# One pinned order for the turn from projection to attention, the last rotation on GpSimd, and first `aT` tiles in memory of their own

## The chip, the cores and the metric

The kernel runs on one core of a Trainium2 chip. The metric is the device time of one execution in microseconds (us). The engines are named as the profile names them: PE is TensorE's matmul, PEld its weight load, DVE is VectorE, ACT is ScalarE, POOL is GpSimd and SP is SyncE, which here only issues DMAs.

## What is computed

One layer of a diffusion backbone with 1024 latent tokens and 256 context tokens of width 1024, all in float32. A combined input projection feeds two groups of heads, retention and differential attention; their outputs go through one output projection, and a gated MLP with a small convolution follows. The change concerns the start of the differential attention. Its queries get a rotation by position, and each of the 4 heads has two score maps, whose softmaxes are subtracted:

```python
def apply_rope(x, cos, sin):
    half = x.shape[-1] // 2
    x1, x2 = x[..., :half], x[..., half:]
    ...
    return jnp.concatenate([x1 * cs - x2 * sn, x1 * sn + x2 * cs], axis=-1)
...
    def attend(qb):
        s = jnp.einsum('bhmqd,bhmkd->bhmqk', qb, k).astype(jnp.float32) * scale
        p = jax.nn.softmax(s, axis=-1)
        a = p[:, :, 0] - lam * p[:, :, 1]
        return jnp.einsum('bhqk,bhke->bhqe', a.astype(v.dtype), v)
...
    n = of * lax.rsqrt(jnp.mean(of * of, axis=-1, keepdims=True) + EPS)
```

The last line is the norm of each attention output over its 128 values.

## The kernel before, in words

Products at full precision are made of three passes (`passes`, L132 to L134): a high and a low part of each operand, high with high, high with low, low with high, gathered in one PSUM tile.

The input projection is made block by block. Its last block, the queries of the differential attention, goes through `transposed`: for each head and each half of the 1024 tokens, one PSUM tile `pl` (128 features x 512 tokens) is gathered from 8 x 3 = 24 matmuls, and `rotated` turns it: four ACT copies of 32 rows put the swapped halves into `xb` (L443), DVE multiplies the tile by the cosine into `xa` (L446) and `xb` by the sine (L447) and adds them (L448). Then `split_store` casts the sum into its high part on ACT (L434), takes the low part on DVE (L435), both in `xhl`, and SP stores them to `dq_d` in device memory (L436). `xa`, `xb` and `xhl` come from a pool named `er`. The last two tiles, both of head 3, are called qa (first half of the tokens) and qb (second half) here. Head 0's queries have been stored long before and are loaded back as `qhl` (L974), its keys as `ks` (L979) and its values as `va` (L982), all issued on POOL.

Attention has 32 units, 4 heads x 8 tiles of 128 queries. The operations of a unit are methods of `Unit`, with one letter each: S, for either of two maps (S1 before S0), makes six matmuls of scores into a PSUM tile `pA` (L890); M reduces them to a minimum on DVE (`mt`, L893), E takes the exponential on ACT with its sum (`p`, `sa`, L897). R and C on DVE work out the ratio of the two sums and combine the two maps (L905). T turns the combined map in three groups, 0, 1 and 2, of four, four and two PE transposes into `pt` (L910), K copies each group to `aT` on ACT (L916), V multiplies it by the values into `pv` (L922). O copies the result to `oa` (L926), Q squares it on ACT (L931) and makes `e` on POOL (L933); f ends the norm's factor on DVE (L936) and with a power on POOL (`ssa`, L937), n scales `oa` on ACT (L940), and Y, h and l turn and split it into `yT`. `pt`, `pv` and Y's `pty` share two PSUM banks (tag "s"), so a T can start only when an earlier tile of theirs has been copied out. `aT`, `oa`, `e`, `ssa` come from a pool `at`.

What sets the order: the numbers of `TAU` place each operation of a unit in periods of one unit, the loop issues them in that order, and `in_order` pins PE, DVE, ACT and SP to the order in which the instructions are written; the order on POOL is left to a scheduler. The turn stands ahead of this loop: S1 to C of unit 0 (`EARLY`) and the tiles qa and qb are written one after the other and not pinned, so the scheduler mixes them. The pool `at` is opened when the projection's pools are closed, and lies partly in memory in which `er` was. Each head's keys go in turn to `ak0` and `ak1`, both allocated ahead of the turn.

## Time and profile before

| what | us |
|---|---|
| median of 3 runs | 1398.27 (1397.23 to 1399.22) |
| the profiled execution | 1400.12 |
| its span in the trace | 1398.3 |
| PE busy in the span | 1369.1 |
| input projection and retention end, attention begins | about 450 to 480 |
| first `pv` matmul (unit 0) | 480.18 |

The profile is of one execution, of which each instruction has a start and a duration in us from the span's start. The clock named PEclk is the share of full speed that TensorE was granted. An idle time is put down to what ended it.

### The profile page before, as it was taken

To read this page: it belongs to the slowest core of one execution; us is meant where nothing else is said; L and a number is where in the kernel's file an instruction comes from. 1 tells how busy PE (TensorE), PEld (TensorE's weight loads), DVE (VectorE), ACT (ScalarE), POOL (GpSimd) and SP (SyncE) were. 2 spreads that over 40 slices of the span, in tenths; PEclk is the share of its full clock that TensorE was granted. 3 is DMA by queue.
4 is the path that set the end of the run, shared out by engine and by line. 5 is a ranking of instruction groups with operands and counts; after the bars stand their busy time and mean duration, and the time that the engine had idled before them with its cause. 6 is when DMAs were issued, how large, how long until landed. Compare 5 with 4: busy or idle time off the path is not lost.

```text
span 1398.3 us, 19669 instructions
## 1 busy us (share of the span) xinstructions
PE 1369.1 (98%) x7028; PEld 1148.4 (82%) x7028; DVE 1013.7 (72%) x1516; ACT 740.9 (53%) x1414; POOL 336.0 (24%) x379
## 2 busy tenths in 40 slices
PE   8999999999999899999999999999999999999997
PEld 6788888788888799998887778888888888888886
DVE  5867756523466898886357998877777777998756
ACT  5546444303466789987036545554455555455433
POOL 1310002501446223411101243233322230033003
PEclk9999999999999999999999999999999999999999
DMA  9467987876679578632221223323233225953324
GB/s 383 154 210 246 309 264 247 263 239 185 191 220 228 163 171 181 139 91 75 105 98 45 91 106 113 110 93 113 98 113 113 76 90 211 392 195 102 133 98 150
DMA packets 107114, 230.88 MB, mean 165 GB/s; under 512 B 9541, under 2 KB 42821, under 8 KB 105097
## 3 DMA queue, kind: packets, MB, share of 16 engines
q1 hardware_dynamic: 98888, 204.73, 42.8%
q0 software_dynamic: 8128, 24.91, 8.0%
q8 instruction: 55, 0.90, 0.3%
q14 instruction: 43, 0.34, 0.1%
HBM read 165.37 MB, written 64.23 MB: 164 GB/s over the span
## 4 chain that ended last, share of the span: by engine, by line
PE 48%; DVE 3%; issue 1%; DMA 1%; ACT 0%; POOLq 0%; POOL 0%; DVEq 0%; ACTq 0%
PE c L133 5%; PE chain L132 5%; PE chain L133 5%; PE c L134 5%; PE c L132 5%; PE chain L134 5%; PE third L132 3%; PE third L133 3%; PE third L134 3%; PE po L134 2%; PE po L133 2%; PE po L132 2%; PE second L132 1%; PE second L133 1%; PE second L134 1%; DVE wlo L1064 1%
## 5 line engine op out<-in xcount | busy, mean ns | idle before, releaser
L132 PE MATMUL pl<-hT,whi 128*128 128x512 f32 x256 | 107.5, 420 | 0.0
L134 PE MATMUL chain<-T,wlo 128*128 128x512 f32 x264 | 103.0, 390 | 2.0 <-DVE wlo L1064 2.0
L132 PE MATMUL chain<-T,whi 128*128 128x512 f32 x264 | 103.0, 390 | 1.3 <-ACT ua L1317 1.3
L133 PE MATMUL chain<-T,whi 128*128 128x512 f32 x264 | 102.8, 389 | 0.0
L134 PE MATMUL pl<-hT,wlo 128*128 128x512 f32 x256 | 100.5, 392 | 0.0
L133 PE MATMUL pl<-hT,whi 128*128 128x512 f32 x256 | 100.2, 392 | 0.0
L893 DVE TENSOR_REDUCE mt<-pA 128x1 f32<-128x1280 f32 x64 | 95.4, 1490 | 4.1 <-PE pA L890 3.6
L890 PE MATMUL pA<-ks,qhl 128*128 128x512 f32 (+1 forms) x384 | 90.8, 372 | 2.5 <-ACT p L897 2.5
L443 ACT ACTIVATE xb<-pl 32x512 f32<-32x512 f32 (+1 forms) x96 | 56.7, 590 | 64.2 <-PE pl L134 45.1
L134 PE MATMUL c<-whi,ghl 128*128 128x512 f32 x232 | 90.4, 390 | 0.0
L132 PE MATMUL c<-whi,ghl 128*128 128x512 f32 x232 | 90.3, 389 | 0.0
L133 PE MATMUL c<-wlo,ghl 128*128 128x512 f32 x232 | 90.3, 389 | 0.0
L1212 POOL TENSOR_TENSOR cmb<-wrb 128x512 f32<-128x512 f32 x20 | 28.3, 1414 | 249.5 <-DMA wrb<-w_up 135.2
L897 ACT ACTIVATE p<-pA,mt 128x1280 f32<-128x1280 f32 x64 | 85.4, 1335 | 2.4 <-issue 1.3
L132 PE MATMUL pn<-whi,hT 128*128 128x512 f32 x192 | 85.7, 446 | 0.0
L1063 ACT CAST whi<-cmb 128x512 fp32r<-128x512 f32 x62 | 38.6, 622 | 81.3 <-PE chain L133 63.0
L890 PEld LDWEIGHTS pA<-ks,qhl 128*128 128x128 f32 x384 | 68.4, 192 | 14.4 <-ACT p L897 3.0
L134 PE MATMUL pn<-whi,hT 128*128 128x512 f32 x192 | 76.3, 398 | 1.0 <-POOL hT L608 1.0
L922 PE MATMUL pv<-va,aT 128*128 128x128 f32 x640 | 76.9, 275 | 0.1
L133 PE MATMUL pn<-wlo,hT 128*128 128x512 f32 x192 | 75.9, 396 | 0.0
L922 PEld LDWEIGHTS pv<-va,aT 128*128 128x128 f32 x640 | 74.0, 192 | 0.7 <-DVE yT L951 0.3
L1063 ACT CAST whi<-wra 128x512 fp32r<-128x512 f32 x55 | 33.9, 621 | 71.2 <-PE third L133 42.5
(324 smaller groups left out, 3901.9 us busy)
## 6 DMA issues: line engine op xcount, KB each, us to landing
raw<-w_in SPq DMA_DIRECT2D x32, 512.0 KB, 5.7
wm<-w_mod SPq DMA_DIRECT2D x32, 512.0 KB, 4.8
wra<-w_up SPq DMA_DIRECT2D x24, 512.0 KB, 3.3
wrb<-w_up SPq DMA_DIRECT2D x23, 512.0 KB, 3.5
W<-w_down SPq DMA_DIRECT2D x44, 256.0 KB, 6.2
ad<-s SPq DMA_DIRECT2D x20, 512.0 KB, 3.3
wra<-ad SPq DMA_DIRECT2D x20, 512.0 KB, 3.4
wrb<-ad SPq DMA_DIRECT2D x18, 512.0 KB, 3.7
```

Of the source, the lines that this page charges most:

```text
L132: mm(ps, lh, rh, start=first, stop=False, skip_group_check=more)
L133: mm(ps, lh, rl, start=False, stop=False, skip_group_check=more)
L134: mm(ps, ll, rh, start=False, stop=last, skip_group_check=more)
L443: nc.scalar.activation(xb[q * blk : (q + 1) * blk, :], pt[o : o + blk, :], AF.Copy, scale=scale)
L890: mm(self.pa[m][:, c0:c1], self.q[:, i, m, qs], self.k[:, m, c0:c1], start=(i == 0), stop=(i == 1))
L893: nc.vector.tensor_reduce(out=self.mt[:, m : m + 1], in_=self.pa[m][:, :LK], axis=AX.X, op=ALU.min)
L897: nc.scalar.activation(self.p[m], self.pa[m][:, :LK], AF.Exp, scale=-1.0, bias=self.mt[:, m : m + 1], accum_out=self.s[:, m : m + 1])
L922: mm(self.pv, self.aT[:, c, :], self.v[:, c, :], start=(c == 0), stop=(c == NKT - 1))
L1063: nc.scalar.copy(hi, src)
L1064: nc.vector.tensor_tensor(out=lo, in0=src, in1=r32(hi), op=ALU.subtract)
L1212: nc.gpsimd.tensor_tensor(out=s1, in0=b1, in1=b2, op=ALU.add)
```

## The change

The turn gets an order written out by hand. Units 0, 1 and 2 are created ahead of it, `begin` issues operations of a unit there, and the loop later leaves out what has begun. A class `LastQueries` holds the steps of qa and qb singly: `products` for some of the 8 steps of the gathering, `swapped`, `cosine`, `sine`, `high`, `low`, `store` as before, and two new ones. `copied` takes the whole tile to `xa` in one ACT copy; `rotated_on_gpsimd` swaps the halves with four SP DMAs from `xa` to `xb`, of 32 x 512 floats (64 KB) each, and does the rest in five POOL operations of 128 x 512. qa is rotated as before on ACT and DVE, qb on POOL. `in_order` with the first three of `FORCE` pins PE, DVE and ACT in the turn.

Memory: the `aT` tiles of units 0 and 1 come from a pool `at0` on the other side, which is closed in the loop after step n = 5; `ak1` is allocated there instead, so the keys of head 1 are loaded into memory that the `aT` of unit 1 had. A tile `gap` of 3200 floats per partition stands ahead of `at`, so that `at` no longer lies in the memory of `er`'s tiles, but `oa` lies in that of the rotation tables `rtab`.

```diff
@@ -62,7 +62,6 @@
 SPARE = (16, 4)
 MOD_TICKS = 7
 FIRST_LOADS = (22, 23, 25, 26, 28, 30)
-EARLY = ("S1", "M1", "S0", "M0", "E1", "E0", "R", "C")
 OPS = dict(S="scores", M="least", E="exp", R="ratio", C="combine", T="turn", K="turned", V="values", O="out", Q="square", f="rstd", n="norm", Y="final", h="high", l="low")
 TAU = dict(S0=0.6383, M0=1.1607, E0=1.3358, S1=0.0000, M1=0.2496, E1=0.5394, R=1.5264, C=1.9075, T0=2.7282, K0=2.9894, T1=2.0034, K1=2.3845, T2=2.5020, K2=2.8031, V0=3.2166, V1=3.3979, V2=3.4379, O=3.5960, Q=3.7453, f=4.1465, n=4.3243, Y=4.9985, h=5.1177, l=5.1770)
 FORCE = (mybir.EngineType.PE, mybir.EngineType.DVE, mybir.EngineType.Activation, mybir.EngineType.SP)
@@ -869,13 +868,17 @@
         def loads(name, bufs=1, **kw):
             return aload.enter_context(tc.tile_pool(name=name, bufs=bufs, side="right", reuse_waits="tile", **kw))
 
-        aq0, ak0, av, aq1, al, ak1 = (loads(*args) for args in (("aq0",), ("ak0",), ("av", 2), ("aq1",), ("al", 2), ("ak1",)))
+        aq0, ak0, av, aq1, al = (loads(*args) for args in (("aq0",), ("ak0",), ("av", 2), ("aq1",), ("al", 2)))
+        ak = [ak0]
+        first_aT = ExitStack()
+        at0 = first_aT.enter_context(tc.tile_pool(name="at0", bufs=2, side="right", reuse_waits="tile"))
         pss = {m: loads(f"pss{m}", space=PSUM) for m in (1, 0)}
         n_units = NT * H
         units = {}
 
         class Unit:
             def __init__(self, i):
+                self.i = i
                 self.h, self.qt = divmod(i, NT)
                 self.gain = subg[:, self.h : self.h + 1]
                 self.mt = al.tile([P, 2], F32, name="mt", bufs=3)
@@ -911,7 +914,7 @@
 
             def turned(self, g):
                 if self.aT is None:
-                    self.aT = at.tile([P, NKT, P], F32, name="aT")
+                    self.aT = (at if self.i > 1 else at0).tile([P, NKT, P], F32, name="aT")
                 n = min(4, NKT - 4 * g)
                 nc.scalar.copy(self.aT[:, 4 * g : 4 * g + n, :], self.pt[g][:, :n, :])
 
@@ -965,7 +968,7 @@
                 n = next(behind, None)
                 return nullcontext() if n is None else tc.issue_after(steps[n].pool_ins)
             if qt == 0:
-                cur["k"] = (ak0, ak1)[h % 2].tile([P, 2, LK], F32R, name="ks")
+                cur["k"] = ak[h % 2].tile([P, 2, LK], F32R, name="ks")
             if qt % 4 == 0:
                 cur["q"] = (aq0, aq1)[qt // 4].tile([P, 2, 2, 4 * P], F32R, name="qhl")
             if qt % 4 == 0:
@@ -985,11 +988,95 @@
         warm = al.tile([P, 64], F32, name="warm", bufs=1)
         nc.scalar.activation(warm[:, 0:1], nlam, AF.Exp)
         fore = [load(i) for i in range(3)]
-        units[0] = Unit(0)
-        vars(units[0]).update(fore[0])
-        for op in EARLY:
-            units[0].run(op)
-        transposed(wg, dq_d, rtab, 32, -DIFF_SCALE, 0, by_head[-TAIL:])
+        for i in range(3):
+            units[i] = Unit(i)
+            vars(units[i]).update(fore[i])
+
+        def begin(i, *todo):
+            for op in todo:
+                units[i].run(op)
+                begun.add((i, op))
+
+        class LastQueries:
+            def __init__(self, h, hf):
+                self.h, self.hf = h, hf
+                self.pt = ps_a.tile([P, 512], F32, name="pl", tag="mm")
+                self.xa = er.tile([P, 512], F32, name="xa")
+                self.xb = er.tile([P, 512], F32, name="xb")
+                self.cs, self.sn = (rtab[:, i, hf * 512 : (hf + 1) * 512] for i in range(2))
+
+            def products(self, k0, k1):
+                h = self.h
+                for k in range(k0, k1):
+                    passes(self.pt, wg(k, h * P, (h + 1) * P), tuple(hT[a][self.hf][:, k, :] for a in range(2)), k == 0, k == KD - 1)
+
+            def swapped(self):
+                for q in range(4):
+                    nc.scalar.activation(self.xb[q * 32 : (q + 1) * 32, :], self.pt[(q ^ 1) * 32 : ((q ^ 1) + 1) * 32, :], AF.Copy, scale=-DIFF_SCALE)
+
+            def cosine(self):
+                nc.vector.scalar_tensor_tensor(out=self.xa, in0=self.pt, scalar=-DIFF_SCALE, in1=self.cs, op0=ALU.mult, op1=ALU.mult)
+
+            def sine(self):
+                nc.vector.tensor_tensor(out=self.xb, in0=self.xb, in1=self.sn, op=ALU.mult)
+                nc.vector.tensor_tensor(out=self.xa, in0=self.xa, in1=self.xb, op=ALU.add)
+
+            def high(self):
+                self.hl = er.tile([P, 2, 512], F32R, name="xhl")
+                nc.scalar.copy(self.hl[:, 0, :], self.xa)
+
+            def low(self):
+                nc.vector.tensor_tensor(out=self.hl[:, 1, :], in0=self.xa, in1=r32(self.hl[:, 0, :]), op=ALU.subtract)
+
+            def store(self):
+                c0 = self.hf * 512
+                nc.sync.dma_start(out=dq_d[self.h][:, :, :, c0 : c0 + 512].rearrange("m p a l -> (m p) a l"), in_=r32(self.hl))
+
+            def copied(self):
+                nc.scalar.activation(self.xa, self.pt, AF.Copy, scale=-DIFF_SCALE)
+
+            def rotated_on_gpsimd(self):
+                for q in range(4):
+                    nc.sync.dma_start(out=self.xb[q * 32 : (q + 1) * 32, :], in_=self.xa[(q ^ 1) * 32 : ((q ^ 1) + 1) * 32, :])
+                self.hl = er.tile([P, 2, 512], F32R, name="xhl")
+                for o, a, b, op in (
+                    (self.xa, self.xa, self.cs, ALU.mult),
+                    (self.xb, self.xb, self.sn, ALU.mult),
+                    (self.hl[:, 0, :], self.xa, self.xb, ALU.add),
+                    (self.xa, self.xa, self.xb, ALU.add),
+                    (self.hl[:, 1, :], self.xa, r32(self.hl[:, 0, :]), ALU.subtract),
+                ):
+                    nc.gpsimd.tensor_tensor(out=o, in0=a, in1=b, op=op)
+
+        begun = set()
+        start = len(nc.cur_bb.bb.instructions)
+        qa, qb = [LastQueries(*by_head[i]) for i in (-2, -1)]
+        begin(0, "S1", "M1", "E1")
+        qa.products(0, 4)
+        begin(0, "S0", "M0")
+        qa.products(4, KD)
+        begin(0, "E0")
+        qa.cosine()
+        qa.swapped()
+        begin(0, "R", "C")
+        qb.products(0, 2)
+        begin(1, "S1", "M1")
+        qa.sine()
+        begin(1, "E1")
+        qa.high()
+        qb.products(2, 4)
+        begin(1, "S0", "M0")
+        qa.low()
+        qa.store()
+        begin(1, "E0")
+        qb.products(4, 6)
+        begin(2, "S1", "M1")
+        qb.products(6, KD)
+        qb.copied()
+        begin(2, "E1", "S0")
+        in_order(start, FORCE[:3])
+        qb.rotated_on_gpsimd()
+        qb.store()
         psl.close()
 
     ctx_ya = ctx.enter_context(ExitStack())
@@ -1023,13 +1110,14 @@
 
 
     with ExitStack() as p2:
+        gap = p2.enter_context(tc.tile_pool(name="gap", bufs=1, reuse_waits="tile")).tile([P, 3200], F32, name="gap")
         at = p2.enter_context(tc.tile_pool(name="at", bufs=2, reuse_waits="tile"))
         psa = p2.enter_context(tc.tile_pool(name="psa", bufs=1, space=PSUM, reuse_waits="tile"))
 
         start = len(nc.cur_bb.bb.instructions)
         order = sorted(TAU.items(), key=lambda it: it[1] % 1.0)
         for n in range(n_units + 8):
-            if 0 < n < n_units:
+            if 2 < n < n_units:
                 units[n] = Unit(n)
                 vars(units[n]).update(fore[n])
             if n == 9:
@@ -1041,10 +1129,13 @@
                     nc.gpsimd.dma_start(out=yT[a][i][:, 0:H, :], in_=yr_d[i][:, a])
             for op, t in order:
                 u = n - int(t)
-                if 0 <= u < n_units and (u or op not in EARLY):
+                if 0 <= u < n_units and (u, op) not in begun:
                     units[u].run(op)
                 if op == "f" and n >= 12:
                     next(wo_gen, None)
+            if n == 5:
+                first_aT.close()
+                ak.append(loads("ak1"))
             if n + 3 < n_units:
                 with tc.issue_after(units[n - 5].pool_ins.ins) if n >= 5 else nullcontext():
                     fore.append(load(n + 3))
```

PE at the turn, before, right behind the last products of qb. Numbers are those of tiles: `pA_4732` and `pA_4742` are the scores of unit 1 (S1, S0), `pA_4754` and `pA_4780` those of unit 2, `pA_4797` S1 of unit 3; `pt_4761`, `pt_4772` and `pt_4787` are T1, T2 and T0 of unit 0.

```order
L890 MATMUL pA_4732<-ks_4592,qhl_4593 128x512 x4
L890 MATMUL pA_4732<-ks_4592,qhl_4593 128x256 x2
L890 MATMUL pA_4742<-ks_4592,qhl_4593 128x512 x4
L890 MATMUL pA_4742<-ks_4592,qhl_4593 128x256 x2
L890 MATMUL pA_4754<-ks_4592,qhl_4593 128x512 x4
L890 MATMUL pA_4754<-ks_4592,qhl_4593 128x256 x2
L910 MATMUL pt_4761<-ident_69,p0_4622 128x128 x4
L910 MATMUL pt_4772<-ident_69,p0_4622 128x128 x2
L890 MATMUL pA_4780<-ks_4592,qhl_4593 128x512 x4
L890 MATMUL pA_4780<-ks_4592,qhl_4593 128x256 x2
L910 MATMUL pt_4787<-ident_69,p0_4622 128x128 x4
L890 MATMUL pA_4797<-ks_4592,qhl_4593 128x512 x4
```

And after, from the end of S1 of unit 2 (`pA_4711`) on; `pl_4611` is qb, `pA_4728` S0 of unit 2, and `pt_4779`, `pt_4786` and `pt_4792` are T1, T2 and T0 of unit 0.

```order
L893 MATMUL pA_4711<-ks_4592,qhl_4593 128x256 x2
L131 MATMUL pl_4611<-hT01_172,whi_3792 128x512
L132 MATMUL pl_4611<-hT11_174,whi_3792 128x512
L133 MATMUL pl_4611<-hT01_172,wlo_3793 128x512
L131 MATMUL pl_4611<-hT01_172,whi_3792 128x512
L132 MATMUL pl_4611<-hT11_174,whi_3792 128x512
L133 MATMUL pl_4611<-hT01_172,wlo_3793 128x512
L893 MATMUL pA_4728<-ks_4592,qhl_4593 128x512 x4
L893 MATMUL pA_4728<-ks_4592,qhl_4593 128x256 x2
L913 MATMUL pt_4779<-ident_69,p0_4656 128x128 x4
L913 MATMUL pt_4786<-ident_69,p0_4656 128x128 x2
L913 MATMUL pt_4792<-ident_69,p0_4656 128x128 x4
```

In before all products of qb stand ahead of the scores of units 1 and 2, and T1 and T2 of unit 0 between the two sets of unit 2. Now the sets of units 1 and 2 stand between pieces of the products (S1 of unit 2 ahead of the last six, S0 behind them), and the three T of unit 0 follow one another. Line numbers of after are shifted by a few lines.

ACT in the same place, before; `xb<-pl` is a quarter of a tile's swap, `p_4620` and `p_4622` are E1 and E0 of unit 0, `p_4740` and `p_4768` those of unit 1, `p_4778` E1 of unit 2.

```order
L443 ACTIVATE xb<-pl 32x512
L897 ACTIVATE p_4620,sa<-pA,mt 128x1280
L897 ACTIVATE p_4622,sa<-pA,mt 128x1280
L443 ACTIVATE xb<-pl 32x512 x7
L897 ACTIVATE p_4740,sa<-pA,mt 128x1280
L434 CAST xhl<-xa 128x512
L897 ACTIVATE p_4768,sa<-pA,mt 128x1280
L434 CAST xhl<-xa 128x512
L916 COPY aT<-pt 128x512
L897 ACTIVATE p_4778,sa<-pA,mt 128x1280
L916 COPY aT<-pt 128x256
L916 COPY aT<-pt 128x512
```

And after; the `p` of units 0, 1 and 2 come in the same order of units.

```order
L900 ACTIVATE p_4622,sa<-pA,mt 128x1280
L900 ACTIVATE p_4656,sa<-pA,mt 128x1280
L1015 ACTIVATE xb<-pl 32x512 x4
L900 ACTIVATE p_4683,sa<-pA,mt 128x1280
L1026 CAST xhl<-xa 128x512
L900 ACTIVATE p_4703,sa<-pA,mt 128x1280
L1036 ACTIVATE xa<-pl 128x512
L900 ACTIVATE p_4726,sa<-pA,mt 128x1280
L919 COPY aT<-pt 128x512
L919 COPY aT<-pt 128x256
L919 COPY aT<-pt 128x512
L900 ACTIVATE p_4821,sa<-pA,mt 128x1280
```

Four of the eight swap copies and one cast to `xhl` are gone, one copy `xa<-pl` has come, and E1 of unit 2 stands ahead of the first `aT` copy and no longer behind it.

POOL, whose order the scheduler makes, before, from the loads of head 0 on; `e` and `ssa` first belong to units 0 and 1.

```order
L982 DMA va<-dvd 128x10x128
L974 DMA qhl<-dq_86 64x4x512 x2
L933 TENSOR_TENSOR e<-sa 128x1 x2
L1011 DMA woraw<-w_out 128x512 x4
L937 TENSOR_TENSOR ssa<-ssa,mhalf 128x1
L933 TENSOR_TENSOR e<-sa 128x1
L979 DMA ks<-dk_91 64x2x1280
L974 DMA qhl<-dq_87 64x4x512
L937 TENSOR_TENSOR ssa<-ssa,mhalf 128x1
```

And after.

```order
L985 DMA va<-dvd 128x10x128
L977 DMA qhl<-dq_86 64x4x512 x2
L1049 TENSOR_TENSOR xa<-xa,rtab 128x512
L1049 TENSOR_TENSOR xb<-xb,rtab 128x512
L1049 TENSOR_TENSOR xhl<-xa,xb 128x512
L936 TENSOR_TENSOR e<-sa 128x1 x2
L1049 TENSOR_TENSOR xa<-xa,xb 128x512
L1049 TENSOR_TENSOR xhl<-xa,xhl 128x512
L940 TENSOR_TENSOR ssa<-ssa,mhalf 128x1
L936 TENSOR_TENSOR e<-sa 128x1
L985 DMA va<-dvd 128x10x128
```

The five operations of qb's rotation stand ahead of the power of unit 0 (the first `ssa`), with the first two `e` between them, and the loads of `woraw` have gone further back.

## The prediction

> **What bounds the kernel now.** I read the busy shares first, then the waits of PE in the stretch that the change touches, and then that stretch engine by engine in the timeline.

> ```profile
> PE 1369.1 (98%) x7028; PEld 1148.4 (82%) x7028; DVE 1013.7 (72%) x1516; ACT 740.9 (53%) x1414; POOL 336.0 (24%) x379
> core 0: us, PE busy (x) PEld busy (x) DVE busy (x) ACT busy (x) POOL busy (x), PEclk, DMA share, GB/s
> 454.00:456.00 2.00, 1.91 (x10) 1.65 (x11) 1.53 (x4) 0.87 (x3) 0.03 (x1) 1.00 0.73 231
> 460.00:480.00 20.00, 16.30 (x74) 13.42 (x73) 15.41 (x20) 14.49 (x24) 0.65 (x3) 0.91 0.52 160
> 480.00:500.00 20.00, 20.00 (x155) 18.95 (x153) 18.09 (x24) 17.78 (x40) 7.59 (x15) 1.00 0.96 204
> 470.00:472.00 2.00, 0.85 (x2) 0.76 (x3) 2.00 (x4) 1.60 (x3) 0.00 (x0) 0.81 0.00 0
> 472.00:474.00 2.00, 2.00 (x8) 1.72 (x8) 2.00 (x4) 1.08 (x1) 0.00 (x0) 0.50 0.03 8
> 474.00:476.00 2.00, 1.99 (x11) 1.61 (x9) 2.00 (x4) 0.85 (x3) 0.00 (x0) 0.84 0.67 262
> 476.00:478.00 2.00, 0.66 (x4) 0.42 (x4) 1.86 (x5) 1.48 (x2) 0.00 (x0) 1.00 0.39 153
> ```

> PE is the bound: 98% busy, and 20.00 of 20.00 us once attention runs (480 to 500). The turn, 460 to 480, is an exception, with 16.30. So what PE gains or loses in the turn is kept to the end; nothing behind it has slack on PE to give it back. In the turn two things are lost. One is waits, which stand in brackets in PE's timeline (start, duration, line, tiles, count, idle time before and its releaser):

> ```profile
> 454.09 0.33 PE L312 MATMUL pyt<-ident,y 128*128 128x128 f32 x1 [1.27 <-POOL y L308]
> 454.72 0.40 PE L132 MATMUL pl<-hT,whi 128*128 128x512 f32 x1
> 458.16 1.30 PE L890 MATMUL pA<-ks,qhl 128*128 128x512 f32 x6
> 459.30 0.40 PE L132 MATMUL pl<-hT,whi 128*128 128x512 f32 x1
> ...
> 466.81 2.46 PE L890 MATMUL pA<-ks,qhl 128*128 128x512 f32 x12
> 471.15 2.45 PE L890 MATMUL pA<-ks,qhl 128*128 128x512 f32 x6 [1.87 <-ACT p L897]
> 473.40 1.43 PE L910 MATMUL pt<-ident,p 128*128 128x128 f32 x6
> 474.53 1.46 PE L890 MATMUL pA<-ks,qhl 128*128 128x512 f32 x6
> 477.16 0.66 PE L910 MATMUL pt<-ident,p 128*128 128x128 f32 x4 [1.17 <-ACT aT L916]
> 478.48 1.44 PE L890 MATMUL pA<-ks,qhl 128*128 128x512 f32 x6 [0.66 <-ACT p L897]
> 479.75 0.60 PE L910 MATMUL pt<-ident,p 128*128 128x128 f32 x4
> 480.18 2.40 PE L922 MATMUL pv<-va,aT 128*128 128x128 f32 x20
> ...
> 485.83 2.40 PE L922 MATMUL pv<-va,aT 128*128 128x128 f32 x20
> ...
> 491.60 2.40 PE L922 MATMUL pv<-va,aT 128*128 128x128 f32 x20
> ```

> From 466.81 on these are 1.87 + 1.17 + 0.66 = 3.7 us. The other loss is the clock, the column behind POOL in the windows: 0.81, 0.50 and 0.84 from 470 to 476, right behind the 1.87 us wait. At full clock the same work would have taken 2 x (0.19 + 0.50 + 0.16) = 1.7 us less.

> **The change part by part.** *PE's order.* The same instructions run, but the score sets of units 1 and 2 are laid between the products of the last tile, so exp and reduction run beside products. I lay the new order out from 454.72, where the kernels are still alike, with rates from the rows above. The tiles qa and qb take 48 products of `pl`. From 454.72 to 458.16 there are 15, from 459.30 to 466.81 33: 3.44 + 7.51 = 10.95 us. Score sets between there and the first `pv` are six in either kernel (S0 of unit 0, S1 and S0 of unit 1, S1 and S0 of unit 2, S1 of unit 3), by 458.16 to 459.30 and 2.46 for two about 1.2 each: 7.2 us. Fourteen transposes, four in 0.43 (479.75 to 480.18), make 1.45. Together 19.6, which puts the first `pv` at 474.3. One wait is new. T0 of unit 0 needs the bank that ACT's K1 copy frees, and K1 stands behind E1 of unit 2:

> ```profile
> 472.92 1.33 ACT L897 ACTIVATE p<-pA,mt 128x1280 f32<-128x1280 f32 x1 [1.32 <-issue]
> 476.52 0.59 ACT L916 COPY aT<-pt 128x512 f32<-128x512 f32 x1 [1.67 <-DMA dq<-xhl]
> ```

> The products of qb end at 454.72 + 10.95 + four sets of 1.2 = 470.5. ACT then copies qb out (0.59), runs E1 (1.33) and K1 (0.59), with 0.2 for the hand-over until 473.2. PE reaches T0 after one more set and six transposes at 470.5 + 1.2 + 0.65 = 472.3 and waits 0.9. First `pv`: 474.3 + 0.9 = 475.2 against 480.18, a head start of 5.0 us. It holds 3.7 of waits and 1.7 of clock, less 0.9, and 0.5 of drains at the waits. The 1.27 us wait at 454.09 stays.

> *Memory of its own for `aT`.* It removes the wait [1.67 <-DMA dq<-xhl] of ACT, and POOL's wait of 19.83 us (below); both are in the head start and not counted again. The later key tile of head 1 is off the path: it is for unit 8, and a unit takes 5.8 us (485.83 to 491.60).

> *The rotation on POOL.* This is the price. ACT loses four `xb` pieces and a cast for one copy, DVE loses four operations. Both lay beside PE's products, so I give that no worth of its own. SP issues four DMAs that swap the halves of `xa` into `xb`. All five POOL operations follow, since the first writes `xa`, which these DMAs read. POOL's pow of unit 0 (`ssa`) stands behind them in POOL's order, ACT's norm of unit 0 waits for the pow, and E0 of unit 3 and the K1 copy of unit 2 queue behind the norm on ACT; PE's transposes T2 of unit 2 wait for that copy's bank. ACT's O copy of unit 0 waits for POOL's second operation, which is done (476.9 by the sum below) before its `pv` is (475.2 + 2.4). The rows:

> ```profile
> kvg<-st SPq DMA_DIRECT2D x32, 128.0 KB, 1.9
> dq<-xhl SPq DMA_DIRECT2D x8, 512.0 KB, 3.0
> L429 SPq DMA_DIRECT2D rqk<-xq x8: 360/374/377, 234.9 to 274.2; - x8
> L436 SPq DMA_DIRECT2D dq<-xhl x8: 512/516/526, 410.4 to 476.1; - x8
> L428 POOL TENSOR_TENSOR xq<-xa,qd x16: 1261/1293/2326, 231.4 to 272.9; 128x512 f32<-128x512 f32 x16
> 258.98 2.53 POOL L428 TENSOR_TENSOR xq<-xa,qd 128x512 f32<-128x512 f32 x2 [1.45 <-DVE xa L448]
> 264.47 3.53 POOL L428 TENSOR_TENSOR xq<-xa,qd 128x512 f32<-128x512 f32 x2 [2.96 <-DVE xa L448]
> 479.16 0.33 POOL L933 TENSOR_TENSOR e<-sa 128x1 f32<-128x1 f32 x2 [19.83 <-DMA dq<-xhl]
> 483.83 0.57 POOL L937 TENSOR_TENSOR ssa<-ssa,mhalf 128x1 f32<-128x1 f32 x1 [1.93 <-DVE ssa L936]
> 481.87 1.55 DVE L905 SCALAR_TENSOR_TENSOR p<-p,r,p 128x1280 f32<-128x1280 f32 x1
> L893 DVE TENSOR_REDUCE mt<-pA 128x1 f32<-128x1280 f32 x64 | 95.4, 1490 | 4.1 <-PE pA L890 3.6
> 484.92 0.40 ACT L940 ACTIVATE oa<-oa,ssa 128x128 f32<-128x128 f32 x1
> 486.85 0.58 ACT L916 COPY aT<-pt 128x512 f32<-128x512 f32 x1
> 488.07 0.38 PE L910 MATMUL pt<-ident,p 128*128 128x128 f32 x2
> ```

> The copy of qb ends at 471.2. Before shows no transfer from one part of on-chip memory to another. Its nearest rows are the smallest stores, 1.9 us for 128 KB, and 3.0 for 512 KB; these four are of 64 KB, so I take 1.9. Three issues of 0.36 to 0.52 lie ahead of the last, 1.3 together: landed at 471.2 + 1.3 + 1.9 = 474.4 (475.9 by the upper ends). Five operations at 2.53 / 2 = 1.27, the `e` pair of 0.33 and the pow of 0.57 make 7.25: the pow ends at 481.65 if nothing disturbs it. But the group L428 goes from 1.26 to 2.33 for one shape: the pairs take 2.53 or 3.53, 1.0 more. The same happens here where POOL's operation meets DVE's combine (1.55 us, two operands of `p`, one every 5.8 us); reductions from PSUM lie beside it too, but I charge only combines. In 6.7 us one meeting is likely: 1.0 to 1.07 us, pow at 482.7. None gives 481.65, all five at the longest 487.0.

> The norm stood 484.92 - 480.18 = 4.74 behind the first `pv`, so it would now come at 479.9 and waits 2.8 us for the pow. Behind ACT, PE has 488.07 - (486.85 + 0.58) = 0.64 of slack, so PE loses 2.2. That leaves 5.0 - 2.2 = 2.8 us. The last term is the clock. A wait of 1.87 us was followed by 1.7 us lost to it; the waits of 1.27 and 1.17 were not (the column says 1.00 from 454 and from 476 on). One of 2.2 is longer than the first, so I take the full 1.7; between nothing and 1.7 lies the range. Sum: 2.8 - 1.7 = 1.1 us gained.

> [...]

> The profiled execution took 1400.12 (span 1398.3), 1.85 over the median of 1398.27. The change moves one stretch of a few us, so I take the sum off the median.

> **The rivals.**

> *No meeting, or an earlier pow (faster).* The pow ends at 481.65, ACT stalls 1.75, PE 1.1, which is no more than the waits after which the clock stayed. Gain 5.0 - 1.1 = 3.9: 1394.4. For it: the row of 2.53 shows undisturbed pairs, and the combine is on DVE for only a quarter of the time. Against it: 6.7 us is longer than a period. Chance 0.31.

> *The clock holds.* One meeting, but the wait of PE is followed by no drop, because PE's wait is cut in parts or falls otherwise in time: gain 2.8, 1395.5. For it: 1.17 and 1.27 us did nothing; against it: 1.87 did. Chance 0.15, of which a third counts as faster.

> *Every POOL operation is as slow as the longest (slower).* If POOL and DVE hold each other up throughout, reductions included, five operations take 5 x 2.33 and the pow ends at 487.0. ACT stalls 7.1, PE 6.4, the clock takes 1.7: 6.4 + 1.7 - 5.0 = 3.1 lost, 1401.4. It turns to a loss from a pow at 483.9 on (PE's 3.3 with the clock's 1.7 eats the head start), and to over 0.2% at 486.7. For it: DVE is busy 18.09 of 20 us in 480 to 500. Against it: most of this is reductions of 1.49 us with one operand outside the memory that POOL reads. Chance 0.12.

> *The change doesn't do what it says.* S1 or S0 of unit 2 waits for E1 or E0 of unit 1, since DVE reaches their reductions late: the pieces of qb between the sets (six products, 1.4 us) are about as long as a reduction of 1.49. Each such wait costs up to 0.5, 1 us in all. It would make 1398.2. Chance 0.12.

> **How the numbers follow.** A measurement of this kernel can tell about 0.2%, 2.8 us, from no change. The forecast, one meeting and a dropped clock, 1.1 us gained, is 1397.2 with a chance of 0.30. It, the rival of the late reductions and two thirds of the clock rival are within 0.2%: 0.30 + 0.12 + 0.10 = 0.52. Faster: 0.31 + 0.05 = 0.36. Slower: 0.12. The range goes from 1394.0, the gain of 3.9 with a few tenths of drains, to 1400.0, where swap DMAs that land at 475.9 and a second meeting (1.5 + 1.07 more for PE) come on top of the forecast; what lies beyond is most of the slower case and a little on the fast side, some 0.15 to 0.2.

> **What would show it.** In the profile after: no [.. <-ACT p] wait of PE between 466 and 472; first `pv` near 475.2; the five operations of POOL from about 474.4 to 481 or 482, one of them near 2.3; a norm on ACT with [2 to 3 <-POOL ssa] ahead of it; a wait of PE of 1 to 2.5 near 482 to 486, with or without a clock under 1.00 behind it. A clock of 1.00 throughout, or a PE without a wait there, makes it wrong on the fast side; a pow behind 484 or a wait of POOL for the swap DMAs beyond 476, on the slow side.

## The result, and the profile after

| | us |
|---|---|
| before, median of 12 runs | 1398.89 (1397.23 to 1401.1) |
| changed, median of 12 runs | 1396.88 (1395.3 to 1400.94) |
| ratio of the times | 0.9984 (0.9977 to 0.9991) |
| span of the profiled execution | 1394.9 (before 1398.3) |

The change gained 2.2 us (1.3 to 3.2 by the interval). The forecast was 1.1. I read the profile after in the order of the prediction: first the stretches and the clock, then PE, then what PE waits for. Windows first; the columns are those shown before.

```profile
460.00:480.00 20.00, 19.11 (x113) 16.50 (x112) 18.05 (x20) 14.64 (x27) 5.82 (x6) 1.00 0.48 139
480.00:500.00 20.00, 17.41 (x127) 15.85 (x127) 16.24 (x22) 15.80 (x38) 11.22 (x20) 1.00 0.98 201
482.00:484.00 2.00, 0.32 (x3) 0.12 (x2) 0.42 (x2) 1.37 (x2) 2.00 (x5) 1.00 0.34 134
484.00:486.00 2.00, 1.13 (x6) 1.00 (x7) 1.59 (x2) 2.00 (x5) 1.16 (x2) 1.00 0.70 183
```

The turn from 460 to 480 now has PE busy for 19.11 of 20 us, where it was 16.30. The stretch behind it, full before, has 17.41: part of the gain is given back at 482 to 485. And the clock is 1.00 throughout, ahead of the wait and behind it. PE's timeline shows where:

```profile
452.92 0.33 PE L311 MATMUL pyt<-ident,y 128*128 128x128 f32 x1 [1.28 <-POOL y L307]
...
471.83 0.66 PE L913 MATMUL pt<-ident,p 128*128 128x128 f32 x4 [0.73 <-ACT aT L919]
...
473.92 2.40 PE L925 MATMUL pv<-va,aT 128*128 128x128 f32 x20
...
479.45 0.63 PE L913 MATMUL pt<-ident,p 128*128 128x128 f32 x4 [0.16 <-DVE p L908]
479.92 2.40 PE L925 MATMUL pv<-va,aT 128*128 128x128 f32 x20
484.87 0.44 PE L913 MATMUL pt<-ident,p 128*128 128x128 f32 x2 [2.55 <-ACT aT L919]
...
488.81 2.40 PE L925 MATMUL pv<-va,aT 128*128 128x128 f32 x20
```

The transposes `pyt` ahead of the turn come at 452.92 here and at 454.09 in before, with the same program up to there; the start scatters from execution to execution (452.3 to 455.2 over all profiles of this study). So everything is counted from these transposes. The first `pv` is 21.00 us behind them, in before 26.09: a head start of 5.09. The three waits of 1.87, 1.17 and 0.66 are gone, one of 0.73 has come at T0 of unit 0. The third `pv` is at 488.81, 35.89 behind the transposes, where before had 491.60 - 454.09 = 37.51: of 5.09 only 1.62 is left. That loss of 3.47 is the wait of 2.55 and what hangs on it. On ACT, SP (its line's durations in ns and first and last start), POOL and DVE the cause of it reads so:

```profile
469.40 0.60 ACT L1036 ACTIVATE xa<-pl 128x512 f32<-128x512 f32 x1 [0.68 <-PE pl L133]
482.63 0.40 ACT L943 ACTIVATE oa<-oa,ssa 128x128 f32<-128x128 f32 x1 [3.87 <-POOL ssa L940]
484.24 0.57 ACT L919 COPY aT<-pt 128x512 f32<-128x512 f32 x1
```

```profile
L1040 SPq DMA_DIRECT2D xb<-xa x4: 581/586/611, 470.0 to 471.9; - x4
DMA to landing us min/median/max: 2.0/2.0/2.0
```

```profile
474.10 1.27 POOL L1049 TENSOR_TENSOR xa<-xa,rtab 128x512 f32<-128x512 f32 x1 [16.02 <-DMA xb<-xa]
...
476.68 1.28 POOL L1049 TENSOR_TENSOR xhl<-xa,xb 128x512 fp32r<-128x512 f32 x1
477.92 1.59 POOL L936 TENSOR_TENSOR e<-sa 128x1 f32<-128x1 f32 x2
479.46 1.26 POOL L1049 TENSOR_TENSOR xa<-xa,xb 128x512 f32<-128x512 f32 x1
480.80 1.27 POOL L1049 TENSOR_TENSOR xhl<-xa,xhl 128x512 fp32r<-128x512 f32 x1
482.03 0.57 POOL L940 TENSOR_TENSOR ssa<-ssa,mhalf 128x1 f32<-128x1 f32 x1
```

```profile
475.35 1.27 DVE L905 SCALAR_TENSOR_TENSOR r<-r,sa,nlam 128x1 f32<-128x1 f32 x1
476.65 2.65 DVE L908 SCALAR_TENSOR_TENSOR p<-p,r,p 128x1280 f32<-128x1280 f32 x1
```

The chain is the predicted one: the copy of qb on ACT, four swaps issued by SP, five operations of POOL, unit 0's power, ACT's norm with 3.87 us of idle time ahead of it, E0 and the copy to `aT` (484.24) behind the norm, and PE's transposes that need its bank.

### The profile page after: what moved, and what is told of

It reads as the page before. It is cut to its first block, busy times and chain, and to the rows that moved or that the text cites. A ratio compares the mean times of both kernels' runs of the same rounds, so it can differ in the third digit from the quotient of the medians.

```text
span 1394.9 us, 19667 instructions
## 1 busy us (share of the span) xinstructions
PE 1365.6 (98%) x7028; PEld 1145.1 (82%) x7028; DVE 1016.7 (73%) x1512; ACT 738.9 (53%) x1410; POOL 340.8 (24%) x384
## 4 chain that ended last, share of the span: by engine, by line
PE 61%; DVE 3%; issue 1%; ACT 1%; POOL 1%; DMA 1%; SPq 0%; POOLq 0%; ACTq 0%; DVEq 0%
PE c L132 5%; PE c L133 5%; PE chain L131 5%; PE chain L132 5%; PE chain L133 5%; PE c L131 5%; PE pA L893 5%; PE pv L925 5%; PE third L131 3%; PE third L132 3%; PE third L133 3%; PE pt L913 2%; PE po L133 2%; PE po L132 2%; PE po L131 2%; PE second L132 1%
## 5 line engine op out<-in xcount | busy, mean ns | idle before, releaser
L132 PE MATMUL chain<-T,whi 128*128 128x512 f32 x264 | 102.7, 389 | 0.0
L132 PE MATMUL pl<-hT,whi 128*128 128x512 f32 x256 | 100.3, 392 | 0.0
L132 PE MATMUL c<-wlo,ghl 128*128 128x512 f32 x232 | 90.3, 389 | 0.0
L893 PE MATMUL pA<-ks,qhl 128*128 128x512 f32 (+1 forms) x384 | 89.7, 368 | 0.0
L442 ACT ACTIVATE xb<-pl 32x512 f32<-32x512 f32 (+1 forms) x88 | 52.0, 590 | 60.0 <-PE pl L133 41.3
L893 PEld LDWEIGHTS pA<-ks,qhl 128*128 128x128 f32 x384 | 67.9, 189 | 11.5
L132 PE MATMUL pn<-wlo,hT 128*128 128x512 f32 x192 | 75.4, 393 | 0.0
## 6 DMA issues: line engine op xcount, KB each, us to landing
raw<-w_in SPq DMA_DIRECT2D x32, 512.0 KB, 5.6
wm<-w_mod SPq DMA_DIRECT2D x32, 512.0 KB, 4.7
wra<-w_up SPq DMA_DIRECT2D x24, 512.0 KB, 3.3
wrb<-w_up SPq DMA_DIRECT2D x23, 512.0 KB, 3.4
ad<-s SPq DMA_DIRECT2D x20, 512.0 KB, 3.3
wra<-ad SPq DMA_DIRECT2D x20, 512.0 KB, 3.4
wrb<-ad SPq DMA_DIRECT2D x18, 512.0 KB, 4.7
```

Source lines behind the costliest of these rows:

```text
L132: mm(ps, lh, rl, start=False, stop=False, skip_group_check=more)
L442: nc.scalar.activation(xb[q * blk : (q + 1) * blk, :], pt[o : o + blk, :], AF.Copy, scale=scale)
L893: mm(self.pa[m][:, c0:c1], self.q[:, i, m, qs], self.k[:, m, c0:c1], start=(i == 0), stop=(i == 1))
```

## Experiments

The theory after the result: PE gets a head start from order and memory together, and loses most of it to the power behind the rotation. The rivals: the gain is the memory alone; the rotation had to leave ACT and DVE; the gain is only the clock. One measure serves all kernels beside the time: the **turn**, from the start of the transposes ahead of it to the fifth `pv`, when all of them have gone over to a unit every 5.75 us. Starts in us; "halved" counts the stretches of about 3.4 us at a clock of 0.50 between 448 and 512, in windows of a quarter us.

| kernel | transposes | fifth pv | turn | halved | time against before |
|---|---|---|---|---|---|
| before | 454.09 | 503.11 | 49.02 | 1 | |
| before again | 453.14 | 503.72 | 50.58 | 2 | |
| changed | 452.92 | 500.33 | 47.41 | 0 | 0.9984 (0.9977 to 0.9991) |
| changed again | 452.43 | 499.82 | 47.39 | 0 | |
| 1: power ahead of two operations | 453.91 | 499.91 | 46.00 | 0 | 0.9971 (0.9960 to 0.9981) |
| 2: rotation on ACT and DVE | 452.56 | 500.28 | 47.72 | 1 | 0.9976 (0.9967 to 0.9985) |
| 2 again | 453.03 | 500.73 | 47.70 | 1 | |
| 3: one operation thrice | 453.03 | 501.86 | 48.83 | 0 | 0.9993 (0.9984 to 1.0002) |
| 4: memory only | 452.66 | 500.95 | 48.29 | 1 | 0.9987 (0.9978 to 0.9996) |
| 5: power ahead of three operations | 452.32 | 497.02 | 44.70 | 0 | 0.9965 (0.9952 to 0.9978) |
| 6: order only | 454.47 | 505.14 | 50.67 | 2 | 1.0011 (1.0002 to 1.0020) |
| 9: one operation thrice, power held | 455.24 | 507.56 | 52.32 | 2 | 1.0016 (1.0007 to 1.0024) |

### 1. The power ahead of two operations

```diff
 for op, t in order:
     ...
         units[u].run(op)
+        if u == 0 and op == "f":
+            tc.add_manual_dep(rot[3].ins, units[0].pool_ins.ins.name, ...)
```

`rot` holds the five POOL operations. The fourth is put behind unit 0's power, and the fifth reads what the fourth writes.

> The changed kernel, with one more order on POOL: the fourth and fifth operation of the last tile's rotation stand behind unit 0's power. Theory (the head start of PE is eaten by ACT's norm, which waits for the power behind all five operations): the power follows DVE's step f at 479.5 and ends at 480.1, in place of 482.6, ACT's wait of 3.87 us falls to about 1.4, PE's wait of 2.55 us to 0.2 or less, and the time falls by 1.5 to 2.5 us against the changed kernel, 3.7 to 4.7 against the kernel before. The low end is if the two late operations then meet DVE's next combine. Rival (the rest of the turn, DVE's lengthened combine of unit 2, holds PE anyway): PE waits as long, put down to DVE, and the time is that of the changed kernel within 0.7 us.

POOL's power and PE's waits in this kernel:

```profile
480.62 0.57 POOL L940 TENSOR_TENSOR ssa<-ssa,mhalf 128x1 f32<-128x1 f32 x1
```

```profile
483.92 0.44 PE L913 MATMUL pt<-ident,p 128*128 128x128 f32 x2 [0.62 <-ACT aT L919]
488.30 2.50 PE L925 MATMUL pv<-va,aT 128*128 128x128 f32 x20 [0.29 <-DVE yT L954]
```

The power ends 481.19 - 453.91 = 27.28 behind the transposes, 2.4 earlier than in the changed kernel (482.60 - 452.92 = 29.68). PE's wait falls from 2.55 to 0.62, not to 0.2, and the turn is 1.4 us shorter. The time came down by 1.8 us against the changed kernel (0.9971 and 0.9984 of before; the two intervals overlap a little, so the turn shows it better than the time). The place of the loss is shown: only the power's place on POOL was moved. What is left of it has another reason: ACT's norm still stands idle for 1.48 us ahead of the power, and POOL's `e` pair ahead of that power still takes 1.59 beside DVE's combine of 2.66.

### 2. The rotation on ACT and DVE

```diff
-        qb.copied()
-        begin(2, "E1", "S0")
+        begin(2, "E1")
+        qb.cosine()
+        qb.swapped()
+        begin(2, "S0")
+        qb.sine()
+        qb.high()
+        qb.low()
         in_order(start, FORCE[:3])
-        qb.rotated_on_gpsimd()
         qb.store()
```

> The changed kernel's order and memory, but the last tile is rotated on ACT and DVE as the tile before it is, not on POOL. Theory (POOL's rotation costs PE 2.5 to 3.5 us, through the power): that wait is gone. ACT's four pieces, 2.4 us in place of a copy of 0.6, stand ahead of the first aT copy, so PE's wait at T0 of unit 0 grows from 0.73 to about 2.7, and ACT's cast costs it little more. In sum 0.5 to 1.5 us faster than the changed kernel. Rival (the rotation had to leave ACT and DVE, both nearly full behind the turn, to gain anything): they never catch up, and it is 1 us or more slower than the changed kernel, near the kernel before.

PE's waits, and the clock behind them:

```profile
473.05 0.44 PE L913 MATMUL pt<-ident,p 128*128 128x128 f32 x2 [2.53 <-ACT xb L1015]
```

```profile
474.00:476.00 2.00, 2.00 (x9) 1.60 (x7) 0.96 (x2) 1.65 (x3) 1.18 (x3) 0.57 0.07 16
```

The wait is of the size expected, though at T2 and not T0: what ended it is ACT's last swap copy out of qb's `pl`. The wait at 482 to 485 is gone. But the clock halves behind the new one, to 0.50 from 474.3 to 477.7. The turn is 47.72, no shorter than that of the changed kernel, and the interval of its time (0.9967 to 0.9985) overlaps with the changed kernel's, so the expected gain over it isn't shown. The rival falls that the rotation had to leave ACT and DVE: the new order and memory gain as much with the rotation left there. A second profile of the same kernel was to show whether the halved stretch was chance:

> The second experiment once more, one look. It had a wait of 2.53 us right behind the projection's products and a stretch at half clock behind it; the changed kernel has had a wait of 2.55 us at T2 of unit 2, without such a stretch, in two looks and in the third experiment. Theory (the stretches lie freely against the program, so each of these is chance): the stretch is there or not, 47.7 us of turn with it, 46.0 without. Rival (behind the products a wait of this length halves the clock each time, behind attention's matmuls it doesn't): 47.7 again.

```profile
473.52 0.44 PE L913 MATMUL pt<-ident,p 128*128 128x128 f32 x2 [2.53 <-ACT xb L1015]
```

It came again, at 0.50 from 474.6 to 478.0, with a turn of 47.70, as the rival had it.

### 3 and 9. One operation of the rotation done three times

```diff
                     (self.hl[:, 0, :], self.xa, self.xb, ALU.add),
+                    (self.hl[:, 0, :], self.xa, self.xb, ALU.add),
+                    (self.hl[:, 0, :], self.xa, self.xb, ALU.add),
```

> The changed kernel, with the third operation of the rotation on POOL done three times in place of once: two more operations of 1.27 us ahead of unit 0's power, same result. Theory: the power ends 2.5 us later, at 485.1, ACT's wait goes from 3.87 to 6.4, PE's from 2.55 to 5.1, and the time is 2.5 us above the changed kernel's at a clock of 1.00. Rival on the clock (a wait of some length halves it, as behind the 1.87 us wait of before): up to 1.7 us more, 4.2 above, with a clock under 1.00 in the windows behind the wait. Rival on the place (the power isn't what PE waits for): under 0.5 us.

```profile
479.58 2.60 POOL L1051 TENSOR_TENSOR xhl<-xa,xb 128x512 fp32r<-128x512 f32 x2
482.14 0.57 POOL L940 TENSOR_TENSOR ssa<-ssa,mhalf 128x1 f32<-128x1 f32 x1
...
488.61 0.57 POOL L940 TENSOR_TENSOR ssa<-ssa,mhalf 128x1 f32<-128x1 f32 x1 [1.51 <-DVE ssa L939]
```

```profile
484.98 0.44 PE L913 MATMUL pt<-ident,p 128*128 128x128 f32 x2 [2.55 <-ACT aT L919]
490.25 2.50 PE L925 MATMUL pv<-va,aT 128*128 128x128 f32 x20 [1.01 <-DVE yT L954]
```

This was a miss of the experiment, not of the theory: the order on POOL is left to the scheduler, which put the power of unit 0 behind the extra two and ahead of the last two operations, so just as many stood ahead of it. The power ended at the same distance, PE's wait stayed 2.55, and 1.4 us were lost a unit later, where PE waited 1.01 for DVE, behind POOL's last two operations (1.28 us from 483.89 and 1.37 from 485.74). Experiment 9 holds the power behind all seven.

```diff
+        if u == 0 and op == "f":
+            tc.add_manual_dep(units[0].pool_ins.ins, rot[-1].ins.name, ...)
```

> As the third experiment (the third operation of the rotation done three times on POOL), and now unit 0's power is held behind all seven operations; there it had slipped ahead of the last two. Theory: the power ends 2.6 to 2.8 us later than in the changed kernel, PE's wait at T2 of unit 2 goes from 2.55 to 5.1 to 5.3, the turn from the transposes to the fifth pv from 47.4 to 50.0 to 50.2, the time to 2.2 to 3.0 us above the changed kernel, at full clock. Rival on the clock (an idle of 5 us leaves a stretch of 3.4 us mostly idle wherever it lies, so the next one runs at half): a stretch of 3.4 us at 0.50 follows the wait and another 1.7 us go. Rival on the place (the power isn't the gate): under 0.7 us.

```profile
489.89 0.69 PE L913 MATMUL pt<-ident,p 128*128 128x128 f32 x2 [5.27 <-ACT aT L919]
```

```profile
490.00:492.00 2.00, 2.00 (x6) 1.70 (x7) 1.34 (x2) 1.97 (x6) 0.00 (x0) 0.50 1.12 239
```

PE's wait went from 2.55 to 5.27, by 2.72 for two operations of 1.3: what POOL did ahead of the power counted in full. The time was 0.9984 to 1.0016 of before, 4.5 us more, and the turn 4.9 more: the rival on the clock was right here, with 0.50 from 488.6 to 495.4, two stretches in place of the one that it had named; PE still stood idle for the first 1.3 us of them.

### 4. The memory only

The kernel before, with `at0`, the later `ak1` and the `gap` as in the change's diff, and nothing else of it.

> The kernel before, with only the memory of the change: the first two aT in a pool of their own, the second head's keys allocated after it, the gap. Order and rotation are those of before. Theory (order and memory both count): ACT's first aT copy no longer waits 1.67 us for the store, PE's waits of 1.17 and 0.66 behind it shrink or go, 1.2 to 1.8 us faster than before; the wait of 1.87 and the halved clock stay. Rival (the memory is all of the change's gain): 2.2 us or more faster. Rival (the copy's wait was hidden): no difference within 0.5 us.

```profile
469.71 1.89 PE L894 MATMUL pA<-ks,qhl 128*128 128x512 f32 x6 [1.87 <-ACT p L901]
475.57 1.43 PE L894 MATMUL pA<-ks,qhl 128*128 128x512 f32 x6 [0.33 <-ACT p L901]
...
479.97 0.44 PE L914 MATMUL pt<-ident,p 128*128 128x128 f32 x2 [0.30 <-ACT aT L920]
```

```profile
473.31 0.58 ACT L920 COPY aT<-pt 128x512 f32<-128x512 f32 x1
```

ACT's first `aT` copy waits for nothing. PE's wait of 1.17 is gone, that of 0.66 is down to 0.33, one of 0.30 has come behind the first `pv`; the one of 1.87 and a halved stretch stayed. The time was 1.8 us under before (0.6 to 3.1), the turn 0.7 to 2.3. So the memory gains on its own. The times don't rule out the rival that it is all of the change's gain, since 2.2 lies in that interval.

### 5. The power ahead of three operations, small tiles of their own

```diff
+        small = loads("small", 2)
...
-                self.o = at.tile([P, P], F32, name="oa")
+                self.o = small.tile([P, P], F32, name="oa")
...
+        if op == "f" and u in {0: 2, 1: 4}:
+            tc.add_manual_dep(rot[{0: 2, 1: 4}[u]].ins, units[u].pool_ins.ins.name, ...)
```

`ssa`, `jka` and `e` come from `small` too.

> The changed kernel, with oa, e, ssa and the square's output in a small pool of their own (so they wait for no memory of the rotation), and POOL's third to fifth operation of the rotation put behind unit 0's power, the fifth behind unit 1's too. Theory (the power behind the rotation is what PE loses 3.5 us to; it came down to half of that when two operations were moved): PE's waits of 2.55 and of the first experiment's 0.62 and 0.29 go, the wait of 0.73 at T0 of unit 0 stays; from the transposes ahead of the turn to the fifth pv 44.3 to 45.2 us, against 47.41 in the changed kernel and 46.00 with two operations moved; 0.7 to 1.7 us faster than that, about 4.5 to 6 faster than the kernel before. Rival (DVE's combine, lengthened by POOL, takes the place of the power): PE waits 1 us or more for DVE, and the time is that of the first experiment within 0.5.

```profile
471.23 0.66 PE L914 MATMUL pt<-ident,p 128*128 128x128 f32 x4 [0.74 <-ACT aT L920]
485.40 2.50 PE L926 MATMUL pv<-va,aT 128*128 128x128 f32 x20 [0.26 <-DVE yT L955]
```

```profile
477.73 0.57 POOL L941 TENSOR_TENSOR ssa<-ssa,mhalf 128x1 f32<-128x1 f32 x1 [1.75 <-DVE ssa L940]
```

```profile
474.75 1.25 DVE L906 SCALAR_TENSOR_TENSOR r<-r,sa,nlam 128x1 f32<-128x1 f32 x1
476.04 1.55 DVE L909 SCALAR_TENSOR_TENSOR p<-p,r,p 128x1280 f32<-128x1280 f32 x1
```

POOL now waits for DVE ahead of the power and no longer the other way round, the turn is 44.70, and the time 4.9 us under before (3.1 to 6.7, from 5 runs): the fastest version of this study, by its median 2.7 us under the changed kernel. DVE's `r` still takes 1.25 in place of 0.22 beside a POOL operation, but PE waits for DVE no more than 0.26, so that rival falls. Two things were changed here and not tried apart: besides the later operations, POOL's first `e` now runs at 468.19, ahead of the rotation, as its tile is out of the rotation's memory.

### 6. The order only

Experiment 2 with the memory of before: `aT` from `at`, no gap, `ak1` from the start.

> The order of the change without its memory: aT comes from the pool that lies over the rotation's tiles, there is no gap, the second head's keys are allocated from the start, and the last tile is rotated on ACT and DVE (as in the second experiment). Theory (the new order needs the memory: the first aT copy waits until the last tile's store has landed, 3.0 us behind a store that follows DVE's last step near 475): PE waits 4 us or more at T0 of unit 0, with the first pv 27 to 29 us behind the transposes ahead of the turn (26.09 before, 21.0 changed), and the time is 0 to 3 us above the kernel before. Rival (the order is worth something by itself): 1 us or more faster than before.

```profile
474.94 0.44 PE L910 MATMUL pt<-ident,p 128*128 128x128 f32 x2 [2.52 <-ACT xb L1012]
478.43 1.12 PE L910 MATMUL pt<-ident,p 128*128 128x128 f32 x4 [3.05 <-ACT aT L916]
```

```profile
477.79 0.86 ACT L916 COPY aT<-pt 128x512 f32<-128x512 f32 x2 [0.80 <-DVE xhl L1026]
```

The first `pv` comes 482.20 - 454.47 = 27.73 behind the transposes, in the range expected, and the time is above that of before; PE's wait at T0 is 3.05 and not 4, behind one of 2.52 at T2. What ACT's first `aT` copy waits for is not the store, as I had it, but DVE's last step, behind a cast that the scheduler put ahead of the copy. The order alone loses 1.5 us (0.3 to 2.8), the memory alone gains 1.8 (0.6 to 3.1), both together gain 3.4 (2.1 to 4.6) in experiment 2 with the rotation left where it was: they depend on each other.

### 7 and 8. Both kernels once more

> The kernel before once more, one look. Theory (the clock is judged in stretches of 3.4 us whose start is free against the program; a wait of 1.87 us halves the next stretch only if it lies in one of them): the waits of 1.87, 1.17 and 0.66 come again within 0.1, the halved stretch of 3.4 us comes again or not, and if not, the turn from the transposes to the fifth pv takes 47.3 us in place of 49.02. The transposes ahead of the turn start anywhere from 452.5 to 454.2, as in the six profiles so far, since what is ahead of them scatters by over 1 us. Rival (a wait of 1.87 at this place halves the clock each time): 49.0 again.

```profile
470.19 1.83 PE L890 MATMUL pA<-ks,qhl 128*128 128x512 f32 x6 [1.87 <-ACT p L897]
476.19 0.66 PE L910 MATMUL pt<-ident,p 128*128 128x128 f32 x4 [0.90 <-ACT aT L916]
477.51 2.25 PE L890 MATMUL pA<-ks,qhl 128*128 128x512 f32 x6 [0.66 <-ACT p L897]
```

```profile
472.00:474.00 2.00, 1.87 (x8) 1.40 (x7) 2.00 (x3) 1.89 (x3) 0.00 (x0) 0.50 0.16 62
478.00:480.00 2.00, 2.00 (x9) 1.71 (x8) 0.66 (x2) 1.63 (x3) 1.60 (x5) 0.50 0.00 0
```

> The changed kernel once more, one look. Theory (as above): the wait of 2.55 us comes again within 0.1; whether a stretch of 3.4 us at half clock follows depends on where the stretches lie; the turn from the transposes to the fifth pv takes 47.4 us without it, about 49.1 with it. Rival (at this place the clock holds): 47.4.

```profile
484.37 0.44 PE L913 MATMUL pt<-ident,p 128*128 128x128 f32 x2 [2.56 <-ACT aT L919]
```

The kernel before has one halved stretch in one profile and two in the other, the second behind waits of only 0.90 and 0.66; its turn goes from 49.0 to 50.6. The stretch behind 1.87 came both times, and in experiment 4 too, as the rival had it; that there would be a second one, neither had. The changed kernel has none in either profile, as its rival had it. The turn of before is therefore 1.6 to 3.2 us longer than the changed one, which holds the 2.2 that was timed. By an estimate from the clock of 0.50, a halved stretch of 3.4 us in which PE is busy costs half its length, 1.7 us; without them before would stand at 47.3 and 47.2, and the changed kernel stands at 47.4. By this estimate the change as it is gains nothing at equal clock: what order and memory bring, POOL's rotation takes, and what is left over is the clock that didn't fall in these profiles. That isn't shown. Each run has a mean granted clock: at 0.997 and 0.998 five runs of the changed kernel have a mean time of 1397.4 and 18 of before 1399.0, so some gain may be left at equal clock; these runs were taken at different times, and the mean doesn't say where the clock fell. The changed kernel's clock doesn't hold in every run either: of its 12 runs, five had a mean clock of 0.999 and took 1395.3 to 1396.8 us, two had 0.996 and took 1399.7 and 1400.9.

## Why the prediction was right, and where it was off

The time lies in the range, and the difference from before is under 0.2%, as the forecast had it. By its own steps:

- **PE's order: right.** Head start 5.0 forecast, 5.09 measured; the new wait at T0 0.9 and 0.73; the sets of units 1 and 2 wait for nothing, so the rival of late reductions fell.
- **The chain of the price: right in each link**, from the swaps to the bank of T2.
- **The swaps: too early by 0.9 us.** "Three issues of 0.36 to 0.52 lie ahead of the last", says the forecast: an issue took 0.6, so the last began 1.9 behind the copy and not 1.3. Landing took 2.0 for 1.9, and POOL began 21.18 behind the transposes, where 474.4 stood for 474.4 - 454.09 = 20.31.
- **The meeting of POOL and DVE: about the right size (1.26 for 1.0 to 1.07), another place.** None of POOL's five operations was lengthened (1.26 to 1.28). DVE's `r` and combine were the longer ones (1.27 for 0.22, 2.65 for 1.55), and so was POOL's small `e` pair (1.59 for 0.33); `r` ended with POOL's second operation, and the `e` pair 0.2 behind the combine. Why operations of the two engines grew beside each other no run shows: what was measured is that `r` took about the 1.27 of the POOL operation beside it, and that the combine, beside the next one and the `e` pair, grew by 1.1.
- **The power and PE's loss: mis-sized.** With both, the power ended 1.07 later than forecast (29.68 behind the transposes against 482.7 - 454.09 = 28.61), and ACT waited 3.87 for 2.8. Of this wait PE was spared 1.3 (3.87 - 2.55), not the 0.64 of the forecast. PE still lost 3.47 where 2.2 was forecast: 2.55 at T2, 0.16 for the late combine, the rest in the units around it, which I had not counted.
- **The clock: wrong.** "One of 2.2 is longer than the first, so I take the full 1.7": nothing was lost behind 2.55 us, in two profiles and in experiment 3. This is the step that failed: it priced a wait by its length, while in the traces it is the idle time within one step of a grid of 3.4 us that goes with the halving (1.87 us whole within one in before, 1.34 and 1.21 in two in the changed kernel; last section). It made up for the step above by luck: 2.2 + 1.7 = 3.9 forecast, 3.47 measured. The rival "the clock holds" was what happened, with a larger loss of PE. The time that I gave that rival, a gain of 2.8, and my own 1.1 lie on either side of the 1.6 that the turns of the two profiles show.
- **The kernel before can lose more in the turn than its one profile showed.** Its clock fell there once in the execution I read and twice in the next, so the sum can be too small by up to 1.7 us, by the estimate of half a stretch. One profile doesn't show how often a stretch is halved.

## What to carry to other kernels

When work is moved to an idle engine, look at the small step that already stands in that engine's queue: here a 0.57 us power behind five operations of 1.27 took back 3.47 of the 5.09 us that the new order and memory had won, and moving it ahead of three of them, with small tiles out of the way, gave most of it back. Look also for the memory that a new order will wait for: here the order alone lost time, and with memory of its own it gained. A wait of TensorE can cost more than its length (here 1.87 us were followed by a stretch of 3.4 us at 0.50 in each of three profiles, an estimated 1.7 us more), so a change that takes away short waits is to be priced with the clock behind them, from more than one profile.

## What the runs showed of the hardware

```profile
273.25:273.50 0.25, 0.25 (x3) 0.25 (x3) 0.00 (x0) 0.00 (x0) 0.25 (x1) 0.52 1.06 377
276.50:276.75 0.25, 0.25 (x2) 0.23 (x2) 0.10 (x1) 0.00 (x0) 0.00 (x0) 0.66 1.02 340
471.00:471.25 0.25, 0.10 (x1) 0.11 (x1) 0.25 (x1) 0.25 (x3) 0.00 (x0) 0.96 0.00 0
1392.75:1393.00 0.25, 0.00 (x0) 0.00 (x0) 0.00 (x0) 0.25 (x1) 0.17 (x2) 0.66 0.13 41
```

```profile
1391.50:1391.75 0.25, 0.00 (x0) 0.00 (x0) 0.00 (x0) 0.00 (x0) 0.00 (x0) 0.72 1.02 393
```

- Counted in this way from the halved stretches, the wait of 1.87 lay whole within one step of the grid in all three profiles that have it, and 2.35 to 2.53 us of idle time lay within one in experiments 2 and 6. The changed kernel's wait of 2.55 was split into 1.34 and 1.21 us; where the boundaries lay in the other two profiles without a halved stretch behind such a wait was not shown. So in these profiles the idle time within one step goes with the halving, and the same kernel can be hit or spared: before had one halved stretch in the turn in one profile and two in the other. The exact rule stays open: 1.56 us in two pieces were followed by a halved stretch (second profile of before), and so were 1.3 us in one piece, in a stretch already at 0.50 (experiment 9); 1.34 in one piece were not (changed kernel), and no run moved a wait against the boundaries. That the clock is judged in such stretches is the theory of the expectations; what decides it was not shown.
- Four transfers of 64 KB within on-chip memory, issued one after the other by SP, took 0.58 to 0.61 us of issue each and landed 2.0 us after it.
